# Long convolutions on one Trainium2 core: fp32 transforms against three fp32r products of split parts

## The chip, the cores and the metric

The kernel runs on one core of a Trainium2 chip. The metric is the time of one execution in device microseconds (us), the median of three runs. TensorE (PE) does the matrix products, VectorE (DVE) and ScalarE (ACT) the elementwise work, GpSimd (POOL) small work and some DMA issues, SyncE (SP) most DMA issues.

## The reference, cut to what matters

The program is four blocks of a network on 512 tokens of width 1024. The second one mixes the tokens by long convolutions: two in a row, each over the whole sequence, each gated. The convolution is done through a transform:

```python
k_f = jnp.fft.rfft(k2, axis=0)
u_f = jnp.fft.rfft(u.astype(jnp.float32), n=2 * L, axis=1)
y = jnp.fft.irfft(u_f * k_f[None], n=2 * L, axis=1)[:, :L]
...
z = v
for o, gate in enumerate((x1, x2)):
    z = gate * bidir_long_conv(z, filt[:, o, 0], filt[:, o, 1], filt_bias[o])
return z @ w_out
```

Everything is fp32. The spectra of the filters are computed earlier in the kernel and lie in HBM.

## The kernel before, in words

Tile's scheduler orders the instructions of each engine ahead of time, by program order as priority and by its own estimate of durations; on the chip each engine then works through its list in that order. Buffers come from pools of fixed size: `pair` (25 tiles of 128 x 1024, method `p`), `tmp` (15 of 128 x 512, `t`), `wsplit` (8 of 128 x 1024, `w`), `raw` (5), and in PSUM five banks `acc` and three for the rest.

Nearly every product of the kernel is made of three fp32r matmuls (`mm3`): each operand is split into a high part of 12 significant bits, copied by ScalarE, and a low part, subtracted by VectorE (`split`, lines 221 and 222). The long convolutions are the exception: both constants `FF` (forward) and `FI` (inverse) say "fp32" for all of them, so that `fwd_gen` and `inv_gen` use one plain fp32 matmul for each product, which the trace shows as two records.

`hyena` first makes the three projections with `hy_w_in`. For the third, `eo` folds each of the eight channel tiles into an even and an odd half, four transposes bring it position-major (`eoT`), and ScalarE copies it into the tiles `EU`. Then come the tables `tu` (forward) and `ti` (inverse), two tiles of 128 x 1024 each, loaded as they are by `table`. The convolutions are four units: order o = 0 or 1, channel half 0 or 1.

A forward unit (`fwd_gen`) has four frequency tiles `ft`. Each loads its spectrum `KK`, makes eight products (U and Sn of 128 x 512, four matmuls in all, in two PSUM banks) and then the complex product with six VectorE operations: `ya`, `yb`, their sum, `yc`, `yd`, their difference, the last of each pair written into the tile `y`. An inverse unit (`inv_gen`) has four channel tiles `c4`. Each makes eight matmuls of 128 x 256 over all four `ft` into one bank, ScalarE copies half of it (`zc`), VectorE makes the two halves of z and multiplies by the gate, which a DMA on ScalarE's queue has loaded. For o = 0 the result goes through `eo` again into `EU2` (`sink1`), for o = 1 it is split for the output projection (`sink2`).

`run` takes generators in turn, one channel tile and one frequency tile a round:

```python
run(self.fwd_gen(0, 0, EU[0], Y[0]))
run(self.inv_gen(0, 0, Y[0], sink1), self.fwd_gen(0, 1, EU[1], Y[1]))
run(self.inv_gen(0, 1, Y[1], sink1), self.fwd_gen(1, 0, EU2[0], Y[2]))
run(self.inv_gen(1, 0, Y[2], sink2), self.fwd_gen(1, 1, EU2[1], Y[3]))
run(self.inv_gen(1, 1, Y[3], sink2))
```

These five calls are named run 1 to run 5 below; "the stage" is the time from the first forward matmul to the first matmul of the output projection `hy_w_out`, which follows in `resid`.

Of the kernel before, what the change touches and what calls it, by code (L numbers as in the profile page):

```python
# [41 lines left out]
class First:  # L42
    """The first products W^T x after a norm, from x as it is: the factor per token comes after the products. The first
    four tiles of columns are fed tile by tile of x, as they become final."""

    def __init__(self, k, W, cols, scale, shift=None):
        """shift: a shift after the norm and a bias of the products; what both add to the products is left in bias."""
        self.k, self.W, self.cols, self.scale, self.shift = k, W, cols, scale, shift
        self.in_moe = False
        self.R, self.P, self.w, self.bias, self.S, self.n = [], {}, [], None, None, 0  # L50

    def feed(self, k, h=None):
        """Tile k of x is final, or half h of its tokens."""
# [24 lines left out]
    def shifted(self, raw, k0, ci, n):  # L78
        """The shift times four tiles by 256 columns, a quarter of the partitions each."""
# [27 lines left out]
    def tiles(self, rB):  # L107
        """Yields the four products, scaled, in SBUF."""
# [9 lines left out]
    def more(self, cols, rB):  # L118
        """Yields four more."""
# [16 lines left out]
class Base:  # L136
# [29 lines left out]
    def filter_done(self):  # L166
        """The filter's banks go to the products and the rest."""
        self.fctx.close()
        self.xp = self.pool("extra", 2)
        self.banks(self.ctx, acc=AC, misc=8 - AC)  # L170
# [46 lines left out]
    def split(self, src, h, l, scale=None):  # L217
        """src (times a per-partition scale) = h + l, both of 12 significant bits."""
# [13 lines left out]
    def wload(self, dma, n=1024, alloc=None, use=None):  # L232
        """Load n columns per partition and split them."""
# [18 lines left out]
    def wtiles(self, W, K, k0, kt, c0, alloc=None, use=None, q=None):  # L252
        """Chunks of at most 4 k-tiles by 256 columns."""
# [8 lines left out]
    def fm(self, W, c0, ncols, acts, k0=0, kt=8, K=1024):  # L262
        """Feature-major products: yields (tile, PSUM) per 128 columns of W."""
# [13 lines left out]
    def fm2(self, W, c0, ncols, acts, k0=0, kt=8, K=1024, pools=()):  # L277
        """As fm, all columns with half the tokens before the other half: yields (tile, half, PSUM)."""
# [32 lines left out]
    def rstd_from(self, ss, n):  # L311
        """ss: the sums of squares of eight tiles, or tiles whose sum over tiles and partitions is it, per token."""
# [22 lines left out]
    def norm_sb(self, ss, n):  # L335
        """The factor per token: on partitions, and as a row on all partitions."""
# [7 lines left out]
    def norm_half(self, ss, n, h, r, R=None, more=()):  # L344
        """The same for half h of the tokens; the row stays in PSUM unless R is given."""
# [18 lines left out]
    def sq_acc(self, ss, src, h=None):  # L364
        """Square a tile, or half h of its tokens; four at a time are summed over the partitions."""
# [12 lines left out]
    def flow(self, tasks, window):  # L378
        """Tasks (generators) started in order, one a round, at most window of them at a time, a stage a round each."""
# [26 lines left out]
    def range_red(self, w, k):  # L406
        """w modulo 2 pi, in [-pi, pi]."""
# [30 lines left out]
class Mla:  # L438
# [7 lines left out]
    def ada_vec(self, i, nm):  # L446
        """A modulation vector of layer i: 256 of its values in each quarter of the partitions."""
# [58 lines left out]
    def x_in(self):  # L506
        """The input, feature-major, split, and the first norm's factor per token."""
# [53 lines left out]
    def rope_apply(self, out, y, nm, t, nh, u=None):  # L561
        """Rotate y (heads of 64) into both halves of out (heads of 2 x 64)."""
# [12 lines left out]
    def mla_pre(self, r1, H, out):  # L575
        """Latents, and the keys, values and queries of two heads."""
# [98 lines left out]
    def kv(self, g, c, out, done):  # L675
        """Keys and values of two heads, as tasks."""
# [42 lines left out]
    def queries(self, g, cT, out, done):  # L719
        """Queries of two heads, as tasks."""  # L720
# [49 lines left out]
    def attend(self, KP, o, K, V, Q, QP):  # L770
        """Two heads, as tasks of a head and 128 queries."""
# [53 lines left out]
    def resid(self, W, acts, i, g):  # L825
        """x += g * (W^T acts); the squares' sums for the next norm."""
# [30 lines left out]
class Moe:  # L857
# [31 lines left out]
    def router_prep(self, i):  # L889
        """Fold the modulation into the router: scaled weights, and the bias of the shift."""  # L890
# [8 lines left out]
    def router(self):  # L899
        """Router products with tokens on the partitions."""  # L900
# [8 lines left out]
    def moe_pre(self, i):  # L909
        """Before the products that end in x: the shift as a row, the first weights."""  # L910
# [16 lines left out]
    def moe_x(self, i, k):  # L927
        """As each tile of x is final: scale it, and multiply with the router."""
# [17 lines left out]
    def moe_load(self, i, ec, kind):  # L946
        """Load a chunk into a tile of one of three pools."""
# [5 lines left out]
    def chunk_dma(self, raw, i, e, c, q=None):  # L953
        """Two k-tiles of gate and up (c < 4), or a k-tile of down."""
# [116 lines left out]
    def moe_zero(self):  # L1071
        """The row of a product that comes in another way."""
# [44 lines left out]
    def moe_xt1(self, X, a, P):  # L1117
        """Half of a block's tokens' features, feature-major, with the shift."""
# [149 lines left out]
    def pieces(self, src, dst):  # L1268
        """Three bfloat16 pieces whose sum is src."""
# [46 lines left out]
    def overflow(self, i, R, spare):  # L1316
        """Blocks of 128 tokens of the experts that hold more than 128, under a branch. With a spare block
        the first of them is among the experts, and always computed (its slots may all be empty)."""
# [109 lines left out]
        def finish(idx, late):  # L1428
            """The spare block's slots, and the row of each product of each token."""
# [34 lines left out]
    def combine(self, i, C, L, first):  # L1464
        """The sum of each token's products into x; with products to come, half the tokens before the other."""
# [57 lines left out]
FF = 3  # L1523
FI = 15
# [3 lines left out]
class Hyena:  # L1528
# [13 lines left out]
    def filter_gen(self, z, w, tn, nd):  # L1542
# [21 lines left out]
        def taps(o, c2, i):  # L1564
            """Filter responses of a channel tile, split into even and odd taps, position-major."""
# [101 lines left out]
    def eo(self, z, EU, c4):  # L1667
# [7 lines left out]
        for a in range(2):  # L1675
            src = P[:, a * 256:(a + 1) * 256].rearrange("p (j c) -> p j c", j=2)
            hl = [y.rearrange("p (j c) -> p j c", j=2)[:, :, c4 * 128:(c4 + 1) * 128] for y in EU[a]]
            if len(hl) == 1:
                nc.scalar.activation(hl[0], src, AF.Copy)
            else:  # L1680
                self.split(src, *hl)

    def new_eu(self, o):
        return [[self.p("eu", FT)] if FF >> o & 1 else [self.p("euh"), self.p("eul")] for _ in range(2)]

    def fwd_gen(self, o, half, EU, Y):
        nc = self.nc
        v = nc.vector
        for ft in range(4):
# [5 lines left out]
            for a in range(2):  # L1695
                P = self.acc("fu")
                for j in range(2):
                    sl = slice(j * 512 + ft * 128, j * 512 + (ft + 1) * 128)
                    e = [y[:, j * 512:(j + 1) * 512] for y in EU[a]]
                    if FF >> o & 1:  # L1700
                        self.mm(P, self.tu[a][2][:, sl], e[0], j == 0, j == 1)
                    else:
                        self.mm3(P, self.tu[a][0][:, sl], self.tu[a][1][:, sl], *e, j == 0, j == 1)
# [6 lines left out]
            if FI >> (2 * o + half) & 1:  # L1710
                y = self.p("y", FT)
                v.tensor_add(y[:, :512], a1, a2)
                v.tensor_mul(b1, U, K1)
                v.tensor_mul(b2, Sn, K0)
                v.tensor_sub(y[:, 512:], b1, b2)
                Y.append((y[:, :512], y[:, 512:]))
                yield
                continue
            yr = self.p("yr")
            v.tensor_add(a1, a1, a2)  # L1720
            v.tensor_mul(b1, U, K1)
            v.tensor_mul(b2, Sn, K0)
            self.split(a1, yr[:, :512], yr[:, 512:])
            v.tensor_sub(b1, b1, b2)
            yi = self.p("yi")
# [4 lines left out]
    def inv_gen(self, o, half, Y, sink):  # L1730
        nc = self.nc
        for c4 in range(4):
# [4 lines left out]
            for a in range(2):  # L1737
                for ft in range(4):
                    y = Y[ft][a]
                    sl = slice(ft * 256, (ft + 1) * 256)  # L1740
                    if FI >> (2 * o + half) & 1:
                        self.mm(P[:, a * 256:(a + 1) * 256], y[:, c4 * 128:(c4 + 1) * 128], self.ti[a][2][:, sl], ft == 0, ft == 3)
                        continue
# [7 lines left out]
            nc.vector.tensor_mul(z, z, g)  # L1751
# [3 lines left out]
    def table(self, src, split, whole):  # L1755
        """A table and its two parts."""
        w = self.wp.tile([128, 1024], FT, name=self._nm("tab"), tag="w") if whole else self.raw()
        self.nc.sync.dma_start(w, src)
        if not split:
            return None, None, w  # L1760
        h, l = self.w("wh"), self.w("wl")
        self.split(w, h, l)
        return h, l, w

    def hyena(self, norm, F, fill=None):
# [26 lines left out]
        def sink1(ct, z):  # L1792
            if ct % 4 == 0:
                EU2[ct // 4] = self.new_eu(1)
# [524 lines left out]
```

## Time and profile before

| | before |
|---|---|
| median of 3 runs | 2946.41 us (2946.2 to 2952.02) |
| profiled execution, span from first to last instruction | 2939.1 us |
| its mean granted clock of TensorE, share of full speed | 0.983 |
| busy PE, DVE, ACT, POOL over the span | 2806.4, 1914.6, 1300.5, 144.8 us |
| the stage | 816.9 to 939.0 us of the span |
| forward matmul records (tile fu), inverse ones (tile iv) | 128 and 256 |

The page gives the profiled execution's span alone; the median of the timed runs is 7.3 us above it. A record of a matmul lasts longer than the engine is taken by it, since matmuls are pipelined: the time from one start to the next is what counts. In the timeline an entry with "x8" joins eight records, and its second number is their length together.

### The profile page before, as it was taken

The page shows a single profiled execution, that of the slowest core. Times are in us where ns is not written, and L with a number is a line of the kernel's source. Part 1 is how long each engine was busy: PE and PEld are TensorE (multiplying, and loading weights), DVE is VectorE, ACT ScalarE, POOL GpSimd, SP SyncE. Part 2 cuts the span into 40 slices and gives each one's busy share as a digit, 9 for nine tenths or more (in the row PEclk, how much of TensorE's full clock was granted, in tenths as well). Part 3 has the DMA queues.
Part 4 walks back from the last instruction along what each step waited for, and adds up shares of the span by engine and source line. Part 5 has one row for each costly group of instructions (what it writes and reads, how often), then busy time and mean ns, then how long its engine had stood idle before and what let it go on. Part 6 is the DMA issues. An engine that isn't in the chain of part 4 may idle for free.

```text
span 2939.1 us, 38010 instructions
## 1 busy us (share of the span) xinstructions
PE 2806.4 (95%) x14430; PEld 2223.5 (76%) x14430; DVE 1914.6 (65%) x3260; ACT 1300.5 (44%) x2222; POOL 144.8 (5%) x191
## 2 busy tenths in 40 slices
PE   6899988999999799899999999999999999999998
PEld 2666766767866577678887888888878888888887
DVE  5776748986776498579935486264679645484363
ACT  4566746874312488443224354243343224353341
POOL 0111001110000111200000000000000000000000
PEclk8999998999999899999999999999999999999999
DMA  6666368962443498422222223223222332132321
GB/s 209 220 216 218 113 232 283 388 257 76 160 157 127 146 356 338 151 94 79 100 92 89 83 74 108 93 90 97 80 83 83 101 100 86 58 103 93 106 90 47
DMA packets 128148, 416.96 MB, mean 142 GB/s; under 512 B 13888, under 2 KB 24336, under 8 KB 127952
## 3 DMA queue, kind: packets, MB, share of 16 engines
q1 hardware_dynamic: 96128, 335.06, 32.9%
q0 software_dynamic: 12304, 44.58, 4.1%
q10 hardware_dynamic: 19520, 34.76, 3.4%
q8 instruction: 117, 1.92, 0.3%
q14 instruction: 79, 0.65, 0.1%
HBM read 380.78 MB, written 33.56 MB: 141 GB/s over the span
## 4 chain that ended last, share of the span: by engine, by line
PE 61%; DVE 2%; POOL 1%; issue 1%; DMA 0%; ACT 0%; POOLq 0%; DVEq 0%
PE acc L206 46%; PE gu L206 3%; PE f L206 3%; PE v L206 2%; PE dn L206 1%; PE ss L206 1%; PE nh L206 1%; PE xT L1120 1%; PE o L206 1%; DVE pre L1855 0%; PE S L206 0%; PE xT L206 0%; DVE uy L1918 0%; DMA y<-ys,pos 0%; PE bc L206 0%
## 5 line engine op out<-in xcount | busy, mean ns | idle before, releaser
L206 PE MATMUL acc<-X,wh 128*128 128x512 f32 x2432 | 755.8, 391 | 0.8 <-ACT X L221 0.7
L222 DVE TENSOR_TENSOR wl<-raw,wh 128x1024 fp32r<-128x1024 f32 (+1 forms) x338 | 411.2, 1220 | 408.2 <-ACT wh L221 396.6
L221 ACT ACTIVATE wh<-raw 128x1024 fp32r<-128x1024 f32 (+2 forms) x362 | 370.2, 1027 | 449.5 <-PE acc L206 376.0
L206 PEld LDWEIGHTS acc<-X,wh 128*128 128x128 f32 x2432 | 454.8, 188 | 97.6 <-issue 2.2
L206 PE MATMUL acc<-X,wl 128*128 128x512 f32 x1216 | 473.9, 390 | 0.0
L206 PEld LDWEIGHTS acc<-X,wl 128*128 128x128 f32 x1216 | 228.4, 188 | 47.1
L222 DVE TENSOR_TENSOR wl<-pre,wh 128x1024 fp32r<-128x1024 f32 x184 | 222.0, 1223 | 31.0 <-ACT wh L221 27.2
L206 PE MATMUL acc<-f,wh 128*128 128x512 f32 (+1 forms) x912 | 228.7, 349 | 0.0
L221 ACT ACTIVATE wh<-pre 128x1024 fp32r<-128x1024 f32 x184 | 191.4, 1058 | 37.3 <-PE gu L206 33.2
L206 PEld LDWEIGHTS acc<-f,wh 128*128 128x128 f32 x912 | 157.0, 189 | 25.2 <-issue 3.3
L2086 DVE SCALAR_TENSOR_TENSOR cfa<-sb,par,cfa 128x511 f32<-128x511 f32 (+15 forms) x240 | 163.2, 733 | 1.8 <-ACT cfa L2081 1.8
L206 PE MATMUL acc<-xr,wh 128*128 128x512 f32 x448 | 138.9, 391 | 0.0
L206 PE MATMUL acc<-f,wl 128*128 128x512 f32 (+1 forms) x384 | 136.4, 355 | 0.0
L1918 DVE SCALAR_TENSOR_TENSOR uy<-acc,par,uy 128x511 f32<-128x511 f32 (+1 forms) x128 | 95.7, 748 | 58.5 <-ACT uy L1914 56.3
L206 PE MATMUL f<-xr,wh 128*128 128x256 f32 x640 | 126.7, 291 | 1.8 <-ACT xr L224 1.8
L206 PE MATMUL gu<-wh,xh 128*128 128x512 f32 x264 | 112.1, 425 | 1.9 <-ACT wh L221 1.9
L206 PEld LDWEIGHTS f<-xr,wh 128*128 128x128 f32 x640 | 102.1, 192 | 13.5 <-issue 9.1
L206 PE MATMUL gu<-wl,xh 128*128 128x512 f32 x264 | 106.3, 403 | 0.9 <-DVE wl L222 0.8
L206 PE MATMUL gu<-wh,xl 128*128 128x512 f32 x264 | 106.6, 404 | 0.0
L206 PEld LDWEIGHTS acc<-xr,wh 128*128 128x128 f32 x448 | 83.9, 188 | 18.4 <-issue 1.2
L206 PE MATMUL f<-xr,wl 128*128 128x256 f32 x320 | 91.1, 286 | 0.0
L206 PE MATMUL acc<-xr,wl 128*128 128x512 f32 x224 | 87.6, 391 | 2.4 <-DVE wl L222 2.4
(511 smaller groups left out, 5153.9 us busy)
## 6 DMA issues: line engine op xcount, KB each, us to landing
pre<-in_moe SPq DMA_DIRECT2D x184, 512.0 KB, 8.1
raw<-in_w_in SPq DMA_DIRECT2D x106, 512.0 KB, 3.3
raw<-in_ada_w SPq DMA_DIRECT2D x96, 512.0 KB, 5.0
raw<-in_w_up SPq DMA_DIRECT2D x88, 512.0 KB, 3.3
raw<-in_w_down SPq DMA_DIRECT2D x40, 512.0 KB, 3.4
ys<-Y POOLq DMA_DIRECT2D x28, 512.0 KB, 7.1
raw<-in_hy_w_in SPq DMA_DIRECT2D x22, 512.0 KB, 3.6
kd<-K ACTq DMA_DIRECT2D x32, 256.0 KB, 2.5
```

The costliest lines, as they stand in the source:

```text
L206: return self.nc.tensor.matmul(o, a, b, start=st, stop=sp)
L221: nc.scalar.activation(h, src, AF.Copy)
L222: nc.vector.tensor_sub(l, src, h.bitcast(FT))
L1120: self.nc.tensor.matmul(P[:, k * 128:(k + 1) * 128], X[:, (a * 4 + k) * 128:(a * 4 + k + 1) * 128], self.ident, is_transpose=True, start=k ...
L1918: nc.vector.scalar_tensor_tensor(y[:, d:], src[:, :512 - d], taps[d], y[:, d:], op0=OP.mult, op1=OP.add)
L2086: v.scalar_tensor_tensor(c[j][:, d:], glu[i][:, :512 - d], self.pc(f"cf_conv_w{l}", (30 - d) * 4 + i), c[j][:, d:], op0=OP.mult, op1=OP.add)
```

## The change

All transforms become three fp32r products: `eo` splits each half into a high part (ScalarE) and a low part (VectorE), so `EU` and `EU2` take twice the tiles; `table` loads each table and splits it into two `wsplit` tiles, eight in all; the complex product's two results are split too, and each frequency tile now leaves two tiles, `yr` and `yi`. The sum and the difference of the complex product and the multiplication by the gate move from VectorE to GpSimd. The tables of the forward transforms are let go before the last inverse unit. Nothing else of the program changes (the full difference has comment lines besides).

```diff
-FF = 3
-FI = 15
...
             hl = [y.rearrange("p (j c) -> p j c", j=2)[:, :, c4 * 128:(c4 + 1) * 128] for y in EU[a]]
-            if len(hl) == 1:
-                nc.scalar.activation(hl[0], src, AF.Copy)
-            else:
-                self.split(src, *hl)
-
-    def new_eu(self, o):
-        return [[self.p("eu", FT)] if FF >> o & 1 else [self.p("euh"), self.p("eul")] for _ in range(2)]
+            self.split(src, *hl)
+
+    def new_eu(self):
+        return [[self.p("euh"), self.p("eul")] for _ in range(2)]
...
-                    if FF >> o & 1:
-                        self.mm(P, self.tu[a][2][:, sl], e[0], j == 0, j == 1)
-                    else:
-                        self.mm3(P, self.tu[a][0][:, sl], self.tu[a][1][:, sl], *e, j == 0, j == 1)
+                    self.mm3(P, self.tu[a][0][:, sl], self.tu[a][1][:, sl], *e, j == 0, j == 1)
...
-            if FI >> (2 * o + half) & 1:
-                y = self.p("y", FT)
-                v.tensor_add(y[:, :512], a1, a2)
-                v.tensor_mul(b1, U, K1)
-                v.tensor_mul(b2, Sn, K0)
-                v.tensor_sub(y[:, 512:], b1, b2)
-                Y.append((y[:, :512], y[:, 512:]))
-                yield
-                continue
-            yr = self.p("yr")
-            v.tensor_add(a1, a1, a2)
+            yr, yi = self.p("yr"), self.p("yi")
+            nc.gpsimd.tensor_tensor(a1, a1, a2, op=OP.add)
             v.tensor_mul(b1, U, K1)
             v.tensor_mul(b2, Sn, K0)
+            nc.gpsimd.tensor_tensor(b1, b1, b2, op=OP.subtract)
             self.split(a1, yr[:, :512], yr[:, 512:])
-            v.tensor_sub(b1, b1, b2)
-            yi = self.p("yi")
             self.split(b1, yi[:, :512], yi[:, 512:])
...
-                    if FI >> (2 * o + half) & 1:
-                        self.mm(P[:, a * 256:(a + 1) * 256], y[:, c4 * 128:(c4 + 1) * 128], self.ti[a][2][:, sl], ft == 0, ft == 3)
-                        continue
                     self.mm3(P[:, a * 256:(a + 1) * 256], y[:, c4 * 128:(c4 + 1) * 128], y[:, 512 + c4 * 128:512 + (c4 + 1) * 128],
                              self.ti[a][0][:, sl], self.ti[a][1][:, sl], ft == 0, ft == 3)
...
-            nc.vector.tensor_mul(z, z, g)
+            nc.gpsimd.tensor_tensor(z, z, g, op=OP.mult)
...
-    def table(self, src, split, whole):
-        """A table and its two parts."""
-        w = self.wp.tile([128, 1024], FT, name=self._nm("tab"), tag="w") if whole else self.raw()
-        self.nc.sync.dma_start(w, src)
-        if not split:
-            return None, None, w
-        h, l = self.w("wh"), self.w("wl")
-        self.split(w, h, l)
-        return h, l, w
+    def table(self, src):
+
+        return self.wload(lambda r: self.nc.sync.dma_start(r, src), alloc=self.w)
...
+        self.tu = None
         run(self.inv_gen(1, 1, Y[3], sink2))
-        self.tu = self.ti = None
+        self.ti = None
```

## Rows read from the trace of the kernel before

**Rows 1.** The page's first line.

```profile
span 2939.1 us, 38010 instructions
```

**Rows 2.** Windows: length, busy PE, PEld, DVE, ACT, POOL, then PE clock.

```profile
922.00:939.00 17.00, 13.04 (x52) 10.62 (x52) 10.35 (x19) 4.17 (x8) 0.00 (x0) 0.90 0.34 119
816.90:939.00 122.10, 117.03 (x418) 76.66 (x417) 94.34 (x168) 18.29 (x43) 0.00 (x0) 0.99 0.34 114
700.00:816.90 116.90, 116.81 (x552) 94.50 (x549) 87.31 (x137) 42.55 (x66) 0.00 (x0) 1.00 0.44 156
```

**Rows 3.** By tile: records, ns min/median/max, first and last start.

```profile
L206 PE MATMUL fu<-eu,tab x128: 590/592/697, 816.9 to 918.5; 128*128 128x512 f32 x128
...
L206 PE MATMUL iv<-tab,y x256: 378/379/704, 830.6 to 939.0; 128*128 128x256 f32 x128
L1748 ACT ACTIVATE zc<-iv x16: 365/383/392, 838.6 to 939.5; 128x256 f32<-128x256 f32 x16
```

**Rows 4.** Timeline of TensorE in the stage: start, length, [idle before <-releaser].

```profile
845.01 3.62 PE L206 MATMUL iv<-tab,y 128*128 128x256 f32 x16
848.47 1.02 PE L206 MATMUL fu<-eu,tab 128*128 128x512 f32 x2
849.33 0.60 PE L1674 MATMUL eoT<-par,eo 128*128 128x128 f32 x4
849.76 2.74 PE L206 MATMUL fu<-eu,tab 128*128 128x512 f32 x6
852.34 3.62 PE L206 MATMUL iv<-tab,y 128*128 128x256 f32 x16
...
862.17 2.84 PE L206 MATMUL fu<-eu,tab 128*128 128x512 f32 x6 [0.47 <-ACT eu L1679]
...
927.32 12.05 PE L206 MATMUL iv<-tab,y 128*128 128x256 f32 x46 [3.96 <-DVE yc L1713]
939.01 0.82 PE L206 MATMUL acc<-z,wh 128*128 128x512 f32 x2
```

**Rows 5.** Timeline of TensorE outside the stage: fp32r products of two sizes.

```profile
694.34 0.28 PE L206 MATMUL f<-xr,wl 128*128 128x256 f32 x1
...
694.70 0.28 PE L206 MATMUL f<-xr,wl 128*128 128x256 f32 x1
...
800.33 0.39 PE L206 MATMUL acc<-h,wl 128*128 128x512 f32 x1
...
801.01 0.39 PE L206 MATMUL acc<-h,wl 128*128 128x512 f32 x1
```

**Rows 6.** Timeline of VectorE in the stage.

```profile
835.91 0.69 DVE L1715 TENSOR_TENSOR y<-yc,yd 128x512 f32<-128x512 f32 x1
...
861.13 0.68 DVE L1707 TENSOR_TENSOR ya<-fu,KK 128x512 f32<-128x512 f32 x1
861.73 0.68 DVE L1708 TENSOR_TENSOR yb<-fu,KK 128x512 f32<-128x512 f32 x1
...
904.52 0.41 DVE L1749 TENSOR_TENSOR z<-zc,iv 128x256 f32<-128x256 f32 x1
904.85 0.41 DVE L1750 TENSOR_TENSOR z<-zc,iv 128x256 f32<-128x256 f32 x1
...
906.69 0.69 DVE L222 TENSOR_TENSOR z<-z,z 128x512 fp32r<-128x512 f32 x1 [0.70 <-ACT z L221]
907.30 0.68 DVE L1707 TENSOR_TENSOR ya<-fu,KK 128x512 f32<-128x512 f32 x1
...
919.18 1.22 DVE L222 TENSOR_TENSOR wl<-raw,wh 128x1024 fp32r<-128x1024 f32 x1 [2.32 <-PE fu L206]
...
925.38 0.69 DVE L1707 TENSOR_TENSOR ya<-fu,KK 128x512 f32<-128x512 f32 x1 [1.59 <-DMA KK<-kd]
```

**Rows 7.** GpSimd's groups by line: count, busy us, mean ns.

```profile
L308 POOL TENSOR_TENSOR rq<-vq,mhalf 128x4 f32<-128x4 f32 x16 | 17.2, 1076 | 90.5 <-DVE vq L304 69.9 <-DVE mx L794 20.6
...
L864 POOL IOTA iotas<- 128x512 f32 x1 | 0.6, 556 | 0.4 <-POOLq L2306 0.4
```

More of the change, by code (lines that the diff above doesn't have):

```diff
@@ L1768, in hyena @@
         W = A["hy_w_in"]
-        EU = [self.new_eu(0) for _ in range(2)]
+        EU = [self.new_eu() for _ in range(2)]
         H, late = [], []
@@ L1787, in hyena @@
         del H
-        self.tu, self.ti = ([self.table(A[n][a], f != m, f) for a in range(2)] for n, f, m in (("k_tu", FF, 3), ("k_ti", FI, 15)))
+        self.tu, self.ti = ([self.table(A[n][a]) for a in range(2)] for n in ("k_tu", "k_ti"))
         Z = [None] * KD
@@ L1793, in sink1 @@
             if ct % 4 == 0:
-                EU2[ct // 4] = self.new_eu(1)
+                EU2[ct // 4] = self.new_eu()
             self.eo(z, EU2[ct // 4], ct % 4)
```

## The prediction

> **What bounds the kernel now.** I read the stage by its windows, then by TensorE's timeline, then by what VectorE does beside it. In the stage's 122.1 us TensorE is busy 117.0, VectorE 94.3, ScalarE 18.3 and GpSimd not at all; in the 116.9 us before it TensorE is busy 116.8 and VectorE 87.3 [rows 2]. So TensorE sets both, with VectorE at 77% behind it in the stage. The reader should see that only about 28 us of VectorE lie free there: whatever TensorE gives up beyond that cannot become time.
>
> Of the stage's idle time on TensorE most is one wait: 3.96 us in front of run 5, for the last products of VectorE, after which 46 inverse records take 11.69 us where 9.9 would do at full clock (the window has a granted clock of 0.90, between the levels of 1.2 and 2.4 GHz) [rows 2, 4]. VectorE is late there because a low part of `hy_w_out` stood 2.32 us at its head and a KK load came 1.59 us late [rows 6]. At the turn from run 2 to run 3 TensorE waits 0.47 us for `eu` [rows 4].
>
> **What TensorE saves.** A forward record starts 0.43 us after the one before (six in 2.58 us), an inverse one 0.216 (16 in 3.46) [rows 4]. A product is two records. Three fp32r matmuls of 512 columns take 0.68 us (800.33 to 801.01), of 256 columns 0.36 (694.34 to 694.70) [rows 5]. Forward: 64 products [rows 3] go from 0.86 to 0.68, 55.0 to 43.5 us. Inverse: 128 from 0.432 to 0.36, 55.3 to 46.1. With eight transposes groups of 0.43 [rows 4], 3.4 us, TensorE's work falls from 113.7 to 93.0: 20.7 us saved if nothing else came to bind.
>
> **What the others gain and lose.** VectorE's operations on 128 x 512 start 0.60 us apart, a low part 0.61, those on 128 x 256 0.33 [rows 6]. A frequency tile had six at 0.60 and now has four and two low parts: 3.62 us, no relief. An inverse channel tile loses the gate's 0.60 and gains, for o = 0, two low parts of 128 x 256, 0.66. A round of runs 2 and 3 is then 2.40 + 1.22 + 0.66 (z) + 0.66 (`eo`) + 0.66 = 5.6 us of VectorE against 2.72 + 2.88 + 0.43 = 6.0 of TensorE (before: 7.33, from 845.01 to 852.34 [rows 4]); a round of run 4 is 2.40 + 1.22 + 0.66 + 0.61 = 4.9 against 5.6. TensorE is barely ahead, so latency decides. ScalarE's copies, two a frequency tile, lie in its idle 100 us [rows 2].
>
> GpSimd's price is not in the trace: no such operation of 128 x 512 stands there. Below, an iota of that size, which reads nothing, took 0.56 us; above, three such streams (two read, one written) are 1.67; small TENSOR_TENSORs took 1.08 [rows 7]. I take 1.3, between the small one and the upper end. By the Trainium skill (GPSIMD Engine Reference, section 3.1) an fp32 add of 2048 columns takes 4497 ns there and 2293 on VectorE, by which 512 columns would be an estimated 1.1; the sum would then end 2 to 3 us earlier. No run here shows it.
>
> Nor does a row show whether GpSimd and VectorE hold each other up. At best not; at worst an operation waits out a whole one of the other, 1.3. I take 0.45 a round, a third.
>
> **The sum, along the stage.** Run 1 is set by VectorE: its last y ended at 836.6 [rows 6] and still will, by equal counts, but now the last product is followed by GpSimd 1.3, ScalarE 0.70 (the gap around the copy) and a low part 0.61 [rows 6]: 2.6, and four times 0.45: 841.0. By then TensorE has done run 1 (10.9), one frequency tile of run 2 (2.7; five PSUM banks allow no more) and three quarters of a half inverse (1.1), 14.7 in all, and 78.3 is left: 919.3 with no more waits. To it come:
>
> - Rounds: after `yd` VectorE waits for its own sum to come back, 1.3 + 0.70 less the 1.20 of `yc` and `yd`, 0.8, and the 0.45. A round of runs 2 and 3 becomes 5.6 + 1.25 = 6.85, 0.81 above TensorE's; eight: 6.5. Run 4: 6.15, 0.55 above; four: 2.2.
> - Turns 2 to 3 and 3 to 4: from the last inverse matmul, zc 0.38 [rows 3], z 0.74, GpSimd 1.3, `eo` 0.74, transposes 0.60 [rows 4], high part 0.38, low part 0.41, the second pair 0.33: 4.9, and two products of 0.60 ahead of it on VectorE: 6.1. TensorE fills 3.8 of it (a frequency tile and 1.1). 2.3 each: 4.6.
> - Turn 4 to 5: four products 2.4, GpSimd 1.3, copy 0.70, low part 0.61 and z 0.66 ahead: 5.7. Three banks of partial inverses fill 3.2: 2.5, and the same two late things as now, 2.32 and 1.59: 6.4.
> - Clock: two idle stretches over 3.9 us (before 841.0 and run 5) at the 1.8 us that the one of before cost: 3.6.
> - All eight `wsplit` tiles hold tables, so both first chunks of `hy_w_out` are split after the forward tables go, one more low part of 1.22 in VectorE's list [rows 6]: 1.2. The second pair waits for run 5's end and has 10.9 us of products (48 of 0.227) as cover.
>
> 919.3 + 6.5 + 2.2 + 4.6 + 6.4 + 3.6 + 1.2 = 943.8 against 939.0: 4.8 us longer. Hidden at no cost: the low parts of the first `EU` (16 of 0.33, 5.3 us) and the four table splits, under the projections with their 29.6 free us of VectorE [rows 2]; if that cover failed they would cost up to 10. The table loads have the same bytes on the same queue. `pair` tiles: Y, EU and EU2 double, 24 of 25 are held at run 4's end, so KK comes one tile ahead; before there was room for several.
>
> The profiled execution's span is 2939.1 [rows 1], 7.3 below the median 2946.41; the stage's 4.8 is added to the median: 2951. I round to 2952, since the list orders are made for durations that GpSimd will not keep exactly.
>
> **Rivals.** *TensorE stays the bound.* GpSimd at 0.56 and no holding up: rounds of 6.04, run 1 ends at 838.5, turns of 1.1, run 5's wait 5.0: 838.5 + 78.3 + 2.2 + 5.0 + 3.6 + 1.2 = 928.8, 10.2 shorter: 2936. For it speak VectorE's 5.6 against 6.0; against it that every low part now comes after two other engines. It decides once a round's wait falls under 0.4.
>
> *GpSimd and VectorE exclude each other.* If every GpSimd operation and every VectorE operation with both inputs in SBUF (low parts of y and z, `eo`) run one at a time, two of four VectorE operations a round wait half of 1.3: 1.3 instead of 0.45. 0.85 more in twelve rounds and four frequency tiles of run 1: 13.6; with the 4.8, 18.4 longer: 2965. Nothing in this trace speaks for or against it, since GpSimd is idle in the stage [rows 2]. The Trainium skill (SBUF — State Buffer, section "Who interferes with whom") states just this rule: VectorE's second SBUF input and GpSimd's reads come through one port, held for a whole instruction. No run of before shows it, and it speaks against the change.
>
> *Loads come late.* With KK one tile ahead, one of three rounds waits as at 925.38: four times 1.59, 6.4 more than forecast: 2958. KK's wait at 925.38 speaks for it, the free DMA engines (0.34 busy) against it.
>
> **How the numbers follow.** A difference under 0.2%, 5.9 us, can't be told from none. Forecast case 0.50, by itself 2944 to 2960 (GpSimd 0.56 to 1.67, a wait from 0 to 0.65): 0.26 of it within 0.2%, 0.22 slower, 0.02 faster. TensorE-bound 0.22: 0.19 faster. Exclusion 0.20, slower. Late loads 0.08, 0.07 slower. Faster 0.21, same 0.30, slower 0.49. The range runs from the TensorE-bound time to the exclusion time, a little beyond each: 2934 to 2967.
>
> **What the profile would show.** fu and iv three times as many matmuls at 0.68 and 0.36 a product; TensorE's busy time in the stage down by some 20, its idle time up by as much; a long idle before the first inverse; GpSimd's groups at 0.6, 1.2 or 1.7 us; low parts longer than 0.69 beside GpSimd if the two exclude each other; rounds near 6.9. I am wrong if rounds come out at 6.0 (faster), or over 7.5 (slower), if the orders of the lists put waiting low parts ahead of ready products, or if `hy_w_out` is late at the stage's end.

## The result and the profile after

The change makes the kernel slower: 2992.84 us (median of four runs, 2990.6 to 2994.03) against 2948.78 for the kernel before (2946.2 to 2952.02), a ratio of 1.0145 with a 95% interval of 1.0133 to 1.0157. That is 44 us, where 5 were forecast: the sign is right, the size is far outside the range of 2934 to 2967.

In the profiled execution of before, the stage begins at 816.9 us; in the profiles of the changed kernel and of the sixteen below it begins at 818.1 to 824.8, also where nothing ahead of it differs. So spans mix in some microseconds that the change did not cause, and the text compares a stretch instead: **F**, from the first forward matmul to the last matmul of the output projection. Before it is 986.2 - 816.9 = 169.3. After, the page's first line, the ends of that stretch by tile (ns min/median/max, first and last start) and its two windows (columns as in [rows 2]) are:

```profile
span 2988.8 us, 38539 instructions
```

```profile
L206 PE MATMUL fu<-euh,wh x64: 389/395/796, 824.8 to 956.0; 128*128 128x512 f32 x64
```

```profile
L206 PE MATMUL acc<-z,wl x64: 388/389/628, 983.4 to 1035.4; 128*128 128x512 f32 x64
```

```profile
824.80:982.90 158.10, 118.51 (x610) 99.95 (x609) 99.73 (x168) 39.11 (x75) 60.23 (x46) 0.84 0.28 90
982.90:1035.40 52.50, 49.44 (x209) 37.46 (x208) 18.92 (x23) 20.50 (x28) 4.27 (x2) 0.97 0.46 165
```

F is 1035.4 - 824.8 = 210.6, 41.3 more, nearly the whole difference of the medians. The stage took 158.1 us instead of 122.1 [rows 2]. TensorE's idle time in it rose from 5.1 to 39.6, its granted clock fell from 0.99 to 0.84, and VectorE, barely busier (99.7 against 94.3), was idle for 58.4 instead of 27.8. No engine is the bound of this stage any more. The waits in it, TensorE's first (us in total, times, longest):

```profile
PE iv L206 <- DVE yc L1704: 15.3, 8, 4.0
PE eoT L1672 <- DVE eo L1668: 15.0, 6, 3.8
PE fu L206 <- DVE yc L1704: 3.8, 2, 2.2
PE iv L206 <- DVE yr L222: 2.6, 4, 0.9
```

```profile
DVE z L222 <- ACT z L221: 13.0, 5, 3.4
DVE eo L1668 <- POOL z L1730: 12.6, 8, 2.6
DVE yr L222 <- ACT yr L221: 12.3, 16, 0.9
DVE z L1728 <- ACT zc L1727: 10.3, 5, 2.9
DVE eul L222 <- ACT euh L221: 5.4, 8, 1.0
```

The reader is to see two things. An inverse product that waits for `yc` does not need its value: `yc` is the last reader of a forward PSUM bank, and with five banks the inverse unit's bank is the one that it sets free. And VectorE's first three waits all end on something that went through GpSimd: a gated z on its way to the output projection's split or to `eo`, or the sum that is to be split as `yr`. One round of VectorE in run 2, from one `ya` to the next (start, length, idle before):

```profile
864.51 0.69 DVE L1699 TENSOR_TENSOR ya<-fu,KK 128x512 f32<-128x512 f32 x1
865.61 0.42 DVE L222 TENSOR_TENSOR eul<-eoT,euh 128x256 fp32r<-128x256 f32 x1 [0.41 <-ACT euh L221]
865.95 0.68 DVE L1700 TENSOR_TENSOR yb<-fu,KK 128x512 f32<-128x512 f32 x1
...
867.48 0.68 DVE L1705 TENSOR_TENSOR yd<-fu,KK 128x512 f32<-128x512 f32 x1
868.76 1.38 DVE L222 TENSOR_TENSOR yr<-ya,yr 128x512 fp32r<-128x512 f32 x1 [0.60 <-ACT yr L221]
...
870.73 0.68 DVE L222 TENSOR_TENSOR yi<-yc,yi 128x512 fp32r<-128x512 f32 x1
872.59 0.43 DVE L1668 TENSOR_TENSOR eo<-z 128x256 f32<-128x256 f32 x1 [1.18 <-POOL z L1730]
...
874.07 0.69 DVE L1699 TENSOR_TENSOR ya<-fu,KK 128x512 f32<-128x512 f32 x1 [0.72 <-DMA KK<-kd]
```

It takes 9.56 us where 6.85 were forecast. VectorE's own 5.6 are there, the wait for the sum (0.60, forecast 0.8) and the stretched low part (1.38 for 0.68, forecast 0.45 more) as well. What was not forecast are the wait for the gate (1.18; 2.41 in the next round), for the high part of `eu` (0.41) and for a load (0.72). In run 4 it is worse, since the split of the gated z stands ahead of the next frequency tile in VectorE's list, and TensorE's next inverse waits for the bank behind it:

```profile
946.23 0.69 DVE L222 TENSOR_TENSOR z<-z,z 128x512 fp32r<-128x512 f32 x1 [3.39 <-ACT z L221]
946.83 0.68 DVE L1699 TENSOR_TENSOR ya<-fu,KK 128x512 f32<-128x512 f32 x1
...
948.03 0.68 DVE L1704 TENSOR_TENSOR yc<-fu,KK 128x512 f32<-128x512 f32 x1
```

```profile
948.77 0.58 PE L206 MATMUL iv<-wh,yr 128*128 128x256 f32 x1 [3.88 <-DVE yc L1704]
```

### The profile page after: what moved, and what is told of

It is laid out like the page before. It is cut to its first block, busy times and chain, and to the rows that moved or that the text cites. A ratio compares the mean times of both kernels' runs of the same rounds, so it can differ in the third digit from the quotient of the medians.

```text
span 2988.8 us, 38539 instructions
## 1 busy us (share of the span) xinstructions
PE 2816.7 (94%) x14622; PEld 2251.3 (75%) x14622; DVE 1929.1 (65%) x3280; ACT 1326.0 (44%) x2258; POOL 209.3 (7%) x239
## 4 chain that ended last, share of the span: by engine, by line
PE 57%; issue 3%; DVE 2%; POOL 1%; DMA 1%; ACT 0%; POOLq 0%; DVEq 0%
PE acc L206 46%; PE f L206 3%; PE gu L206 2%; PE v L206 1%; PE ss L206 1%; PE nh L206 1%; PE dn L206 1%; PE o L206 1%; DVE pre L1829 0%; PE S L206 0%; DMA y<-ys,pos 0%; DVE uy L1892 0%; PE xT L1120 0%; PE bc L206 0%; DVE X L222 0%
## 5 line engine op out<-in xcount | busy, mean ns | idle before, releaser
L206 PEld LDWEIGHTS acc<-f,wh 128*128 128x128 f32 x912 | 156.9, 189 | 25.1 <-issue 3.3
L206 PEld LDWEIGHTS acc<-xr,wh 128*128 128x128 f32 x448 | 83.9, 188 | 18.4 <-issue 1.2
L308 POOL TENSOR_TENSOR rh<-vh,mhalf 128x2 f32<-128x2 f32 x18 | 13.3, 736 | 1118.0 <-DVE vh L306 1118.0
```

Source lines behind the costliest of these rows:

```text
L206: return self.nc.tensor.matmul(o, a, b, start=st, stop=sp)
L308: nc.gpsimd.tensor_tensor(r, v, self.mhalf[:, :n], op=OP.pow)
```

## The experiments

The account that came out of the runs: the stage is a ring. Inverse product, zc, z, gate, `eo`, transposes, split, forward product, complex product, split, and back over the PSUM bank; each engine's list holds its members in a fixed order, so that a wait in one is passed on to the others. GpSimd's operations and the split parts lengthen the ring, and TensorE's shorter products do not shorten it. The rivals: VectorE's added work alone (it sets the stage by its length), GpSimd and VectorE holding each other up, late gate loads, too few banks. The expectations number what they weigh: theory 1 is the late gate load, 2 the way through GpSimd, 3 VectorE's added work, 4 the banks, 5 the gate's place at the head of VectorE's list. F and the times of the changed kernel and sixteen others (added F is against 169.3; a ratio without an interval is of one run):

| kernel | F | added | time / before |
|---|---|---|---|
| after | 210.6 | 41.3 | 1.0145 [1.0133, 1.0157] |
| E1 after, gate loads on SyncE | 202.8 | 33.5 | 1.0103 [1.0081, 1.0126] |
| E2 after, sums on VectorE | 207.0 | 37.7 | 1.0132 [1.0110, 1.0153] |
| E3 after, sums and gate on VectorE | 193.6 | 24.3 | 1.0071 [1.0049, 1.0094] |
| E4 before, sums and gate on GpSimd | 174.6 | 5.3 | 1.0018 [1.0005, 1.0031] |
| E5 before, forward products split | 183.7 | 14.4 | 1.0050 |
| E6 before, inverse products split | 183.4 | 14.1 | 1.0051 |
| E7 before, first order's forward products split | 172.9 | 3.6 | 1.0002 [0.9989, 1.0016] |
| E8 after, z and gate after the next frequency tile | 199.5 | 30.2 | 1.0107 [1.0083, 1.0130] |
| E9 after, inverse products in three other banks | 197.2 | 27.9 | 1.0101 |
| E11 E1, E8 and E9 together | 196.9 | 27.6 | 1.0083 [1.0062, 1.0104] |
| E12 after, gate on VectorE | 197.2 | 27.9 | 1.0074 |
| E13 E3 without Y's low parts | 181.0 | 11.7 | 1.0018 |
| E14 after without Y's low parts | 200.5 | 31.2 | 1.0088 |
| E15 E7 with E16's edits | 178.3 | 9.0 | 1.0021 [1.0012, 1.0031] |
| E16 before, other banks and gate loads on SyncE | 172.1 | 2.8 | 1.0006 [0.9996, 1.0016] |
| E17 E3, inverse products in three other banks | 191.1 | 21.8 | 1.0079 [1.0053, 1.0106] |

E7 and E16 cannot be told from the kernel before by their times, though their F is 3.6 and 2.8 us longer: an F within 4 us of another is taken as the same. Added F and added time differ by up to 6 us in kernels timed once (E12: 27.9 and 22; E13: 11.7 and 5), so both are given where they disagree. In the kernels with other banks (E9, E11, E15 to E17) the first output products run ahead of the last inverse ones, so that only F can be compared there, not the stage.

### E1 to E4: GpSimd's part

```diff
# E1
-            nc.scalar.dma_start(g, self.xd[o, ct])
+            nc.sync.dma_start(g, self.xd[o, ct])
# E2; E3 has this and E12's edit
-            nc.gpsimd.tensor_tensor(a1, a1, a2, op=OP.add)
+            v.tensor_add(a1, a1, a2)
...
-            nc.gpsimd.tensor_tensor(b1, b1, b2, op=OP.subtract)
+            v.tensor_sub(b1, b1, b2)
# E12
-            nc.gpsimd.tensor_tensor(z, z, g, op=OP.mult)
+            nc.vector.tensor_mul(z, z, g)
# E4, in the kernel before
-                v.tensor_add(y[:, :512], a1, a2)
+                nc.gpsimd.tensor_tensor(y[:, :512], a1, a2, op=OP.add)
...
-                v.tensor_sub(y[:, 512:], b1, b2)
+                nc.gpsimd.tensor_tensor(y[:, 512:], b1, b2, op=OP.subtract)
...
-            nc.vector.tensor_mul(z, z, g)
+            nc.gpsimd.tensor_tensor(z, z, g, op=OP.mult)
```

> The changed kernel with the gate loads issued by SyncE instead of ScalarE. Theory 1 (the gate load stands behind ScalarE's copy of the GpSimd sum, and each round waits for it: 17.7 us of GpSimd's waits in the stage): the waits for it go, about 15 to 20 us shorter than the changed kernel, 2973 to 2978. Theory 2 (the way through GpSimd itself is too long for the order of TensorE's list, whenever the gate comes): within 4 us of 2993. Theory 3 (VectorE's added low parts bind): within 4 us of 2993.

Measured: F 7.8 us shorter than after's, and 2982 us, between the ranges of both theories. In the changed kernel a gate load is issued from ScalarE's queue just behind the copy of `yr` and lands 2.7 us later (median; 2.5 to 4.5); GpSimd waited 17.7 us for seven of them, and in E1 for none. So a fifth of the loss by F, and somewhat more by the times (1.0145 to 1.0103, some 12 us), is a late load, of the gate and not of KK.

> The changed kernel with the sum and the difference of the complex product on VectorE; the gate stays on GpSimd. Theory 2: the sums' 2.6 us and the 0.5 us by which GpSimd holds the first low part up leave each round, 15 to 30 us shorter than the changed kernel, 2963 to 2978. Theory 1: the copy that the gate load stands behind comes earlier as well, about 10 us shorter. Theory 3: 1.2 us more of VectorE in each of 16 frequency tiles, 2993 or up to 15 us longer.

> The changed kernel with the sums and the gate on VectorE, so the split products alone. VectorE then has 5.6 + 1.2 + 0.6 = 7.4 us a round, as much as TensorE had before (7.33). Theory 2: near the kernel before, 2945 to 2960. Theory 3: 2975 or more. Theory 1: near the kernel before too, since the gate load no longer stands behind a GpSimd sum.

> The changed kernel with the gate alone back on VectorE; the sums stay on GpSimd. Measured from the first forward matmul to the last of the output projection (169.3 us before, 210.6 in the changed kernel). Theory 5 (VectorE stands at the head of its list for GpSimd's gate, 12.6 us in front of eo and 13.0 in front of the low parts of z): it falls to 185 to 192. Theory 2 in its form of the sums (the wait for the sums and the held-up low parts): within 6 us of 210, since the run with the sums on VectorE and the gate on GpSimd took 207.0 and the two are alike.

Measured: the sums' way over GpSimd costs 3.6 us of F with the gate on VectorE (E12 - E3) and 3.6 with it on GpSimd (after - E2), twice no more than F can tell; the intervals of after and E2 overlap as well. The gate's costs 13.4 with the sums on either engine (E2 - E3, after - E12). Together 17.0 of the 41.3. By the ranges E2, at 2990 us, lies nearest to theory 3, E3, at 2971, between theories 2 and 3, and E12, at 197.2, between theories 5 and 2. VectorE's low part of `yr` (min/median/max ns) in the changed kernel, in E2 (sums on VectorE) and in E12 (sums on GpSimd):

```profile
L222 DVE TENSOR_TENSOR yr<-ya,yr x16: 1084/1166/1411, 832.0 to 972.1; 128x512 fp32r<-128x512 f32 x16
```

```profile
L222 DVE TENSOR_TENSOR yr<-ya,yr x16: 680/684/693, 829.9 to 968.1; 128x512 fp32r<-128x512 f32 x16
```

```profile
L222 DVE TENSOR_TENSOR yr<-ya,yr x16: 1075/1170/1417, 828.2 to 960.5; 128x512 fp32r<-128x512 f32 x16
```

GpSimd's second sum holds it up, by 0.48 us in the median and by 8.7 us over all sixteen (19.7 us busy, 11.0 without). Putting the sums back returns only 3.6 of F, since VectorE then has them to do: it is busy 110.4 us in E2's stage, 10.7 more than in the changed kernel. The other 24.3 us are there with GpSimd idle: by F the larger part of the loss, by the times half of it (1.0071 of 1.0145), is the split. Theory 2, by which E3 would come near the kernel before, falls here.

> The kernel before with the sums and the gate on GpSimd, transforms in fp32. Theory 2: the way through GpSimd costs most of the 44 us here as well, 2970 to 2990, though no copy and low part follow the sums. Theory 1: up to 10 us, since the gate load does not stand behind a copy of a GpSimd sum. Theory 3: 2940 to 2950, since VectorE gets 1.8 us a round free.

Measured: in fp32 the same three operations on GpSimd cost 5.3 us, not 17.0, though VectorE waits just as long there (15.7 us for z before `eo`, 13.2 for the split of z). TensorE waited 6.1 us for `y` and 3.2 for `eo`, where the changed kernel has 15.0 for `eo` and 21.7 for `yc` and `yr`. We read it so: TensorE's longer products cover what the split version leaves bare.

### E5 to E7: one transform's split at a time

```diff
# E5; E7 has FF = 2
-FF = 3
+FF = 0
# E6
-FI = 15
+FI = 0
```

> The kernel before with only the forward transforms as three fp32r products (FF = 0), sums and gate on VectorE, Y whole. VectorE has 6.2 us a round against TensorE's 6.6 (7.3 before). Theory 3 (VectorE's work and its latency bind): the stage stays at 118 to 126 us. If TensorE binds still: 112 to 116.

> The kernel before with only the inverse transforms as three fp32r products (FI = 0), sums and gate on VectorE. VectorE has 6.8 us a round with the low parts of Y, TensorE 6.7. Theory 3: the stage grows to 130 to 140 us, most of the 24 that both together cost with everything on VectorE. If the split of Y costs nothing but its own operations: 122 to 126.

Measured: 14.4 and 14.1 more F, in stages of 136.5 and 136.2 us. E6 is inside theory 3's range, E5 is far above both of its ranges. VectorE is busy 101.5 us in E5's stage and 112.8 in E6's, 7.1 and 18.5 more than before. The added times do not follow that added work, so VectorE's length alone isn't the rule either.

> The kernel before with FF = 2: the forward products of the first order alone are three fp32r products (their input U is split in time of the projections, under TensorE's work, so that VectorE has no new work inside the stage beside the two table halves). TensorE has 32 products of 0.18 us less each, 5.8 us. Theory A (the engines wait for each other in turn, and TensorE's length was the cover of that chain): no gain; forward products to last output product takes 169 us or up to 5 more. Theory B (TensorE sets the stage where VectorE gets no new work): 4 to 6 us shorter, 164.

Measured: VectorE is busy 95.6 us in E7's stage, 1.2 more than before, and TensorE has 5.8 us less to do. The time is unchanged (1.0002), as theory A has it. TensorE's timeline shows the first place where the 5.8 went:

```profile
859.84 0.39 PE L206 MATMUL fu<-euh,wl 128*128 128x512 f32 x1
864.64 1.07 PE L1674 MATMUL eoT<-par,eo 128*128 128x128 f32 x4 [3.10 <-DVE eo L1670]
866.18 2.07 PE L206 MATMUL fu<-eu,tab 128*128 128x512 f32 x2 [0.47 <-ACT eu L1679]
```

TensorE ends run 2's products earlier and waits 3.10 us at the turn for `eo` and 0.47 for `eu`; the kernel before has the second of these waits alone [rows 4]. Then the granted clock falls, and two fp32 records take 2.07 where two took 1.02 [rows 4]. Two windows around the wait, and the whole stage (columns as in [rows 2]):

```profile
853.00:869.00 16.00, 12.42 (x50) 9.20 (x49) 14.01 (x25) 3.71 (x7) 0.00 (x0) 0.86 0.48 144
869.00:885.00 16.00, 16.00 (x57) 10.93 (x56) 11.44 (x22) 1.43 (x4) 0.00 (x0) 0.92 0.50 183
821.00:946.70 125.70, 116.39 (x450) 84.85 (x449) 95.58 (x169) 19.43 (x44) 0.00 (x0) 0.95 0.36 119
```

Against the kernel before [rows 2] TensorE is idle 4.2 us longer (9.3 against 5.1), and its busy time falls by 0.6 in place of 5.8, so that by an estimate 5.2 us went to the low clock. The saving went into waits and, about as much, into the clock that fell after them; what the waits alone would have cost no run shows. So even where VectorE got next to no new work, faster products did not shorten the stage: TensorE was the bound of the kernel before with little margin.

### E8, E9, E11, E16, E17: order, banks and queues

```diff
# E8
+            yield
             z = self.t("z")
...
             sink(ct, z)
-            yield
# E9 and E17
-            P = self.acc("iv")
+            P = self.ps("iv")
```

> The changed kernel with z, the gate, eo and the transposes issued after the frequency tile that follows, so that a product of the next frequency tile stands ahead of them in the lists of TensorE and VectorE. If the place of the gate's chain in the lists (15.0 us of TensorE waiting for eo) is what is lost, it is 8 to 14 us shorter than the changed kernel's 210.6 from the first forward to the last output product. If the round's length is set by VectorE's work and its waits for GpSimd whatever the order, within 4 us.

Measured: 11.1 us shorter than after. As much lies in run 4 with its turn, from the first zc of run 4 to the first of run 5 (ScalarE's timeline): 32.1 us here, 43.3 in the changed kernel.

```profile
929.30 0.37 ACT L1728 ACTIVATE zc<-iv 128x256 f32<-128x256 f32 x1
...
961.42 0.38 ACT L1728 ACTIVATE zc<-iv 128x256 f32<-128x256 f32 x1 [0.17 <-PE iv L206]
```

There the gated z is split: VectorE's wait for it before the split fell from 13.0 to 5.9. Runs 2 and 3, which have `eo` and the transposes, are no shorter (41.7 and 41.2 against 40.7 and 41.1). So the number is the first expectation's and the wait is not: the place of waiting work in the lists is worth 11 us, by the split and not by `eo`.

> The changed kernel with the inverse products in the three PSUM banks that the transposes use, instead of the five that the forward products take. Theory 4 (in each round TensorE can start the next inverse only when VectorE's product yc has freed a bank, 19 us of TensorE's idle time in the stage): the stage falls from 158 to 135 to 145 us. Theory 2 (the way through GpSimd and the gate load): the wait moves to the transposes, the stage stays within 5 us of 158.

> The changed kernel with the gate loads on SyncE, the inverse products in the transposes' banks, and the second half of each inverse tile (z, gate, eo, transposes) placed in program order behind the next frequency tile. If order and latency are all that was lost, the stage comes to 105 to 120 us, below the 122 of the kernel before, about 2935 to 2950 in all. If the three engines' work itself is too much (GpSimd's 3.9 us and the low parts that it holds up, a round), it stays at 135 or more, 2965 or more.

Measured: the banks alone give 13.4 us of F, all three edits 13.7 (18 by the times; 2976 us, as the second expectation has it), where they gave 7.8, 11.1 and 13.4 one by one. In E9 the inverse products' wait for `yc` is gone and the wait for `eo` grew from 15.0 to 24.8:

```profile
PE eoT L1672 <- DVE eo L1668: 24.8, 8, 9.0
```

The wait moved to the next link of the ring, as theory 2 had it, and yet time was gained, as theory 4 had it; different edits recover in part the same time.

> All products split, sums and gate on VectorE, and the inverse products in the other three PSUM banks, which takes away the 19.6 us that inverse products waited for a bank to be freed by yc. If VectorE's length sets the stage there (119.6 us busy of 146.4), the waits move to other places and it comes out within 3 us of the run without the banks (193.6 from the first forward to the last output product). If the banks hold the engines in turn, it is 8 to 15 us shorter.

Measured: with all work on VectorE the banks change F by 2.5, as the theory that VectorE sets E3 expects; the 19.6 us that TensorE waited for them there were no loss of their own. TensorE's wait for `eo` rose from 6.6 to 18.4 instead.

> The kernel before with three fp32r products for the forward transforms of o = 0 alone (FF = 2; their splits lie under the projections, so VectorE gets no more to do in the stage), inverse products in the transposes' banks, gate loads on SyncE. If VectorE's added work is what the change lost by, this one loses nothing and TensorE's 5.8 us come through: 161 to 166 us from first forward to last projection matmul, 3 to 8 us less in all than the kernel before. If TensorE's list is the cause, it is slower than before.

> The kernel before with two edits that do not touch the arithmetic: inverse products in the three other PSUM banks, and the gate loaded from SyncE's queue. If the 9.3 us that an earlier run lost (these two edits with the first order's forward products split) belong to the split, this stays within 2 us of the kernel before. If they belong to the banks or the queue (the transposes and the last output products share those three banks, and the list is ordered anew), it is 5 to 10 us longer and the split alone costs little.

Measured: E15 is 0.21% slower than before, and no kernel of this study beat the kernel before. E16, which is E15 without the split, adds 2.8 to F (2.0 by the times, at the edge of its first range); E7, its split alone, adds 3.6; both together 9.0 (9.3 in the expectation). The excess over the sum is 2.6, no more than F can tell; in E15 TensorE waits 13.2 us for `eo` (6 times).

### E13 and E14: Y without its low parts

```diff
-            self.split(a1, yr[:, :512], yr[:, 512:])
-            self.split(b1, yi[:, :512], yi[:, 512:])
+            nc.scalar.activation(yr[:, :512], a1, AF.Copy)
+            nc.scalar.activation(yi[:, :512], b1, AF.Copy)
```

> The run with everything on VectorE, but the low parts of Y are left out: the third product of each inverse takes the high part again, so TensorE's work stays and VectorE loses 32 operations, 19.5 us (the result is not that of the reference). First forward to last projection matmul 193.6 with them. Theory 3 (VectorE's work sets the stage one for one): 172 to 177. If TensorE's list and banks set it: 185 to 194.

> The changed kernel with the low parts of Y left out in the same way; VectorE loses 16 operations of 1.17 us and 16 of 0.68, 29.6 us, and its waits of 12.3 us for the sums. First forward to last projection matmul 210.6 with them. Theory 3 and the exclusion (VectorE's work and what GpSimd holds up): 165 to 175. Theory 5 (the way of the gate): 185 to 200, since eo and the transposes wait for the gate as before.

Measured: E13 takes 19.0 us of work from VectorE (119.7 to 100.7) and gives back 12.6 us of F, between its two ranges; E14 takes 28.8 (99.7 to 70.9, the stretch of `yr` among them) and gives back 10.1, at the edge of theory 5's range. By F the same removal is worth two thirds of its work where VectorE has the most to do and one third where GpSimd stands in the ring. By the times, of one run each, both give back some 16 us, so that the shares are uncertain and only their order stands. VectorE's longest wait in the kernel before, and its waits in E3, beside which E13 is to be read:

```profile
DVE z L1749 <- ACT zc L1748: 13.0, 5, 3.4
```

```profile
DVE z L1728 <- ACT zc L1727: 11.0, 5, 3.1
DVE eul L222 <- ACT euh L221: 5.1, 7, 1.1
DVE yi L222 <- ACT yi L221: 3.5, 5, 0.7
DVE z L222 <- ACT z L221: 2.8, 4, 0.7
```

E3's VectorE is busy 119.7 us in a stage of 146.4 and idle 26.7, almost exactly before's 27.8. The largest piece of what the prediction counted as free is in both the wait for a zc, most of it at the ends of runs, where the first inverse needs the last `y`: VectorE's added work left it nearly as it was (13.0, 11.0). The rest is not the same waits: 8.6 us of E3's are for the high parts of `eu` and `yi`. In the sum, E3's added work (25.3) came out as added time (24.3); that they nearly agree is no rule, since 7.1 and 18.5 of added work made 14.4 and 14.1 in E5 and E6.

## Why the prediction was wrong

Its sum, term by term, against the changed kernel:

- *What TensorE saves.* The products (four of 128 x 512 in a frequency tile) are as forecast: at full clock three starts 0.23 us apart, 0.69 a forward product. The saving never became time, and where the granted clock is at its low level a product takes longer than one of the kernel before did at the high level: starts are 0.43 apart, 1.28 a product, against 0.86 for the fp32 one at full clock [rows 4].

```profile
865.60 0.63 PE L206 MATMUL fu<-euh,wh 128*128 128x512 f32 x1
866.03 0.63 PE L206 MATMUL fu<-eul,wh 128*128 128x512 f32 x1
866.46 0.63 PE L206 MATMUL fu<-euh,wl 128*128 128x512 f32 x1
...
868.53 0.40 PE L206 MATMUL fu<-eul,wh 128*128 128x512 f32 x1
868.77 0.40 PE L206 MATMUL fu<-euh,wl 128*128 128x512 f32 x1
869.00 0.39 PE L206 MATMUL fu<-euh,wh 128*128 128x512 f32 x1
```

  TensorE's busy time was to fall by some 20 us; it is 118.5 against 117.0.
- *GpSimd's price.* 1.3 was taken, and 1.30, 1.28 and 1.37 measured (count, busy us, mean ns). The estimate of 1.1 from the Trainium skill (GPSIMD Engine Reference, section 3.1) was 0.2 short of the sums.

```profile
L1703 POOL TENSOR_TENSOR ya<-ya,yb 128x512 f32<-128x512 f32 x16 | 20.8, 1302 | 172.0 <-DVE yb L1700 169.3 <-issue 2.7
L1706 POOL TENSOR_TENSOR yc<-yc,yd 128x512 f32<-128x512 f32 x16 | 20.5, 1283 | 1.8 <-DVE yd L1705 1.8
L1730 POOL TENSOR_TENSOR z<-z,gate 128x512 f32<-128x512 f32 x14 | 19.1, 1368 | 39.3 <-DVE z L1729 18.9 <-DMA gate<-xd 17.7 <-PE iv L206 2.7
```

- *Run 1.* Its last `y` was forecast 24.1 us after the first forward matmul (841.0 - 816.9); it ended at 849.94, 25.1 after. Right.
- *Rounds*, with the turns: the step that failed. The prediction made a round VectorE's 5.6 plus the wait for its own sum, and compared that with TensorE's 6.04. By its terms run 2, from its first zc to run 3's, is 4 x 6.85 + 2.3 = 29.7 us, run 3 the same, run 4 with its turn and half of the clock's 3.6 is 4 x 6.15 + 6.4 + 1.8 = 32.8. The first zc of runs 2 to 5 (ScalarE's timeline):

```profile
851.36 0.38 ACT L1727 ACTIVATE zc<-iv 128x256 f32<-128x256 f32 x1 [2.15 <-PE iv L206]
...
892.03 0.38 ACT L1727 ACTIVATE zc<-iv 128x256 f32<-128x256 f32 x1 [2.43 <-PE iv L206]
...
933.16 0.38 ACT L1727 ACTIVATE zc<-iv 128x256 f32<-128x256 f32 x1 [2.29 <-PE iv L206]
...
976.43 0.38 ACT L1727 ACTIVATE zc<-iv 128x256 f32<-128x256 f32 x1 [3.18 <-PE iv L206]
```

  40.7, 41.1 and 43.3: the three miss by 11.0, 11.4 and 10.5, 32.9 of the 36.5 us between forecast (4.8) and F (41.3). Three things were left out. The gate's way was counted at the turns alone, though it stands in every round of VectorE's list ahead of the next `ya` (13.4 us by E2 and E3). VectorE's 27.8 idle us were taken as room, when 25.3 us of added work left 26.7 idle and made 24.3 us of time (E3). And the waits of TensorE and VectorE were taken to overlap, as if TensorE could run ahead; that they add up in a ring of five banks and fixed lists is a reading and not shown: E9 speaks for it (13.4 us less with other banks), E17 does not (2.5, where VectorE has the most to do).
- *The clock.* 3.6 us for two stretches were forecast. The stage ran at 0.84: TensorE's two longest groups of waits alone are 14 in number, up to 4.0 us each. Of TensorE's 118.5 busy us some 25 are the low clock's by an estimate (118.5 less the 93.0 of the forecast's products; 0.16 of 158.1 gives the same), and they cost time only where another engine waits for TensorE. VectorE's waits for zc, which follow TensorE's products, did not grow (10.3, 13.0 before). Still, how much of the loss the clock made can't be told apart from the waits: no run here has the one without the other.
- *`hy_w_out`.* 1.2 forecast. The projection took 52.5 instead of 47.2, of which 2.85 and 0.2 are waits for the last z, whose gate ran into a low part of `hy_w_out`, and 2.2 more busy time at a clock of 0.97. GpSimd and VectorE there:

```profile
988.13 2.12 POOL L1730 TENSOR_TENSOR z<-z,gate 128x512 f32<-128x512 f32 x1 [2.19 <-DVE z L1729]
```

```profile
987.91 1.22 DVE L222 TENSOR_TENSOR wl<-raw,wh 128x1024 fp32r<-128x1024 f32 x1
```

Of the rivals, *TensorE stays the bound* is refuted, and by E3 and E7 it would have been without GpSimd too. *Loads come late* named KK: 0.7 us of waiting. The late load was the gate's, whose price the prediction never put down (7.8 by E1). *GpSimd and VectorE exclude each other* is right in its mechanism. The gate at 988.13 lasts until the low part ends (987.91 + 1.22 = 989.13) plus its own 1.28, to within 0.2 us; the `yr` of 868.76 ends 0.55 after GpSimd's sum (868.30 + 1.29), about the 0.60 that such operations start apart. So the rule of the Trainium skill (SBUF — State Buffer, "Who interferes with whom") holds here, at 1.17 us instead of 0.68. It prices at 0.48 a round in the median and 0.55 in the mean, near the forecast's own third (0.45), since VectorE is held up at one low part a round, not at two. It was not what made the size.

That the sign came out right says little: the terms that gave it come to 4.8 us. Two of the prediction's own signs of error came true: rounds over 7.5, and waiting low parts ahead of ready products in the lists (the split of z in run 4).

What stays open: which part of E3's 24.3 us is VectorE's length and which the longer way through high and low parts. E13 removes some of both at once, and gives 12.6. E5 less E7 puts 10.8 on the second order's forward split, whose high and low parts of `eu` lie on the turns' path, but the lists are ordered anew in each build.

## What to carry to other kernels

Where two engines each are busy over three quarters of a stage and feed each other, ask for the length of the whole ring before asking which engine is the bound: write down one round of every engine's list in its order, with every hand-over in it, and count the bank or buffer that closes the ring. Idle time of the second engine is room only if it lies where the new work can run; here 27.8 us were idle, and with 25.3 us of work more (E3) 26.7 still were. Moving an operation to a slower idle engine in the middle of such a ring costs its latency and its hand-overs each round, in this case 17.0 us more than it relieved VectorE by; and a faster product was worth nothing where it only uncovered such waits (E7).

## What the runs showed of the hardware

- A GpSimd operation on SBUF and a VectorE operation with two SBUF inputs ran one after the other, whichever came second: 1084 to 1411 ns for VectorE's 684, and 2.12 us for GpSimd's 1.28 beside a VectorE operation of 1.22. VectorE's products of a PSUM bank with KK kept 679 to 692 ns, also those that ran beside a GpSimd sum (the `yc` of 866.88 beside the sum of 866.78 to 868.06).
- A TensorE wait of 3.1 us, after a stage at full clock, was followed by records at half the rate (two fp32 records of 512 columns in 2.07 us instead of 1.02), and windows at 0.86 and 0.92. In the changed kernel, with TensorE waits of up to 4.0 us in most rounds, the stage ran at 0.84, and an fp32r product at 1.2 GHz took 1.28 us, half as long again as the fp32 product at 2.4 GHz.
